# A decoder trunk in fp32: rotary angles and x*r on GpSimd and ScalarE, an earlier split of the first projections, and seam rows of 320 floats

## The chip, the core and the metric

The kernel runs on one core of a Trainium2 chip. What counts is the time of one execution on the device, in microseconds: the median of several runs. The engines are TensorE (PE; PEld is its weight load), VectorE (DVE), ScalarE (ACT), GpSimd (POOL) and SyncE (SP), which issues most DMAs.

## The reference

A trunk of two layers over 256 tokens of width 1024, batch 1, all in fp32. Each layer's shifts, scales and gates come from a conditioning vector c:

```python
for l in range(DEPTH):
    mod = c_act @ w_ada[l] + b_ada[l]
    shift1, scale1, gate1, shift2, scale2, gate2 = jnp.split(mod, 6, axis=-1)
    hdn = modulate(rmsnorm(x, norm1_g[l]), shift1, scale1)   # h * (1 + scale) + shift
    proj = hdn @ w_in[l]                                     # latents, q/k/v, gates
    ...                                                      # latent, stick-breaking, block attention
    x = x + gate1[:, None, :] * (merged @ w_out[l])
    hdn = modulate(rmsnorm(x, norm2_g[l]), shift2, scale2)
    ff = jnp.square(jax.nn.relu(hdn @ w_ff1[l])) @ w_ff2[l]
    x = x + gate2[:, None, :] * ff
return rmsnorm(x, final_norm_g)
```

Two of the three attentions turn part of q and k by rotary tables, cos and sin of position times frequency. The stick-breaking attention (sb) has none; its scores are z.

## The kernel before

x lies transposed in SBUF: eight slices (k = 0..7) of 128 features by 256 tokens. Weights come in blocks of 1 MB through three buffers `ws`, in a fixed order of jobs; `fetch` issues their DMAs on SyncE. Where a product must be as exact as fp32, each factor is split in a high half in fp32r and a low half that holds the rest, and three fp32r matmuls add up: high by high, high by low, low by high. `split_piece` splits a quarter of a block: ScalarE copies the high half `wh` (L184), VectorE subtracts to get `wl` (L185). Activations go the same way: `high` on ScalarE, `low` on VectorE, into `hh` and `hl` (in the trace both are parts of the tile act).

**The opening** (under `manual_schedule` in `trunk`, so every engine works in the order in which the code is written). VectorE computes the modulation by column: `ada_col` (L1097) multiplies a block of 128x1024 of w_ada by the conditioning row and sums it to one column; a pair of them gives scale (`gs`) and shift (`mod`) of one slice. `scaled(k)` makes x * gs * r on VectorE; for k from 4 on `gained(k)` does it on ScalarE from xr = x * r. The first eight jobs are the stick-breaking q, k and v projections. They run in four groups q of two slices each, as the columns become known: job 2q holds four blocks of the weights (1 MB), job 2q+1 two (0.5 MB). Groups below PLAIN_Q = 2 are plain: activations stay in fp32 (`hf`), weights are used unsplit, and TensorE does fp32 matmuls, each of two passes. Groups 2 and 3 are split. At the end of the opening the fp32 rows `hf` are split too, as later jobs need `hh` and `hl` for all slices.

Between the columns stands the rest: `table_angles`, a generator, which gives angle times frequency (L110), the count of turns (L111, L112), the reduction to one turn in three steps (L115) and a clamp (L116); `tables`, which on ScalarE takes absolute value and two sines and loads two function tables; and x * r for four slices (L1151).

**The seams** (`overlap`; one in the middle of each layer, one between the layers). The next projections start before the norm of x is known: `ahead` writes each new slice times its gain, split, into the tiles xh and xl, whose rows hold 256 tokens and two columns with the shift. `pre_mm` multiplies the weights by these rows of 258, and the norm factor is applied to the result. The sum of squares goes through TensorE: `Rms.sum` adds each term by an fp32 matmul with -1 (ssum), first `acc` with slices 0 to 5 and the late term of slice 6, later that of slice 7.

**The tail** (`tail`) does the last norm: squares of x by tiny matmuls (tsum), transposes of x * g (ft), then the scale. GpSimd multiplies x by the last gain g in the last seam (L813).

## Time and profile before

| what | us |
|---|---|
| median of 3 runs | 935.19 (934.09 to 935.22) |
| the profiled execution | 934.94 |
| its span in the trace | 933.2 |
| TensorE busy | 916.7 (98%) |
| VectorE busy | 731.0 (78%) |
| ScalarE busy | 600.5 (64%) |
| GpSimd busy | 8.7 (1%) |

The profiled execution's own time is 1.74 us above its span and 0.25 below the median of the runs. The busy shares are means over stages that differ: in the opening VectorE's share is higher than its mean, in the body TensorE's is.

### The profile page before, as it was taken

The numbers are of one execution on the slowest core, as the hardware profiler recorded it, in microseconds if no ns is written. First come the engines' busy times: TensorE is split into PE (matmuls) and PEld (weight loads), VectorE is DVE, ScalarE is ACT, GpSimd is POOL, SyncE is SP. The second block draws the span as 40 slices with busy tenths as digits, with TensorE's granted clock in tenths as the row PEclk, the third lists the DMA queues.
The fourth block names the chain that finished last, engine by engine and source line by source line (L and its number), as shares of the span: only waits on it lengthen the run. The fifth ranks groups of instructions, "written<-read, shape, count | busy, mean of one in ns | idle before, by whom it ended". The sixth has DMA issues, their size and how long they took to land.

```text
span 933.2 us, 19188 instructions
## 1 busy us (share of the span) xinstructions
PE 916.7 (98%) x7780; PEld 891.2 (96%) x7781; DVE 731.0 (78%) x1423; ACT 600.5 (64%) x1255; POOL 8.7 (1%) x14
## 2 busy tenths in 40 slices
PE   9999999999999999999999999999999999999997
PEld 6888999899999999999999999989999999999997
DVE  6979789887899986767888877889787989454553
ACT  3577678857676774645566667886667677564642
POOL 0000000000000000000000000000000000000002
PEclk9999999999999999999999999999999999999999
DMA  9956554664767488677947654655666637655531
GB/s 337 401 211 242 168 220 157 221 242 173 256 230 268 143 315 309 228 271 265 341 162 275 226 195 156 218 188 215 236 210 242 219 143 282 255 181 192 179 132 46
DMA packets 34074, 208.77 MB, mean 224 GB/s; under 512 B 3905, under 2 KB 4802, under 8 KB 11458
## 3 DMA queue, kind: packets, MB, share of 16 engines
q1 hardware_dynamic: 33696, 207.09, 62.0%
q8 instruction: 61, 1.00, 0.4%
q10 hardware_dynamic: 146, 0.26, 0.1%
q0 software_dynamic: 144, 0.20, 0.1%
q14 instruction: 27, 0.22, 0.1%
HBM read 206.49 MB, written 1.05 MB: 222 GB/s over the span
## 4 chain that ended last, share of the span: by engine, by line
PE 81%; DVE 9%; DMA 5%; ACT 4%; issue 1%; SPq 0%; DVEq 0%; ACTq 0%
PE ps L349 15%; PE ps L350 15%; PE ps L351 15%; PE ff L984 5%; PE ff L983 5%; PE ff L986 5%; PE pre L371 4%; DVE wl L185 3%; DMA ws<-win 3%; DMA adaw<-wada 2%; ACT wh L184 1%; PE po L476 1%; PE vps L349 1%; PE vps L350 1%; PE vps L351 1%; PE s L531 1%
## 5 line engine op out<-in xcount | busy, mean ns | idle before, releaser
L185 DVE TENSOR_TENSOR wl<-ws,wh 128x512 fp32r<-128x512 f32 (+1 forms) x592 | 378.8, 673 | 132.2 <-ACT wh L184 131.7
L184 ACT ACTIVATE wh<-ws 128x512 fp32r<-128x512 f32 (+1 forms) x592 | 337.3, 615 | 206.1 <-PE ps L350 108.3
L349 PE MATMUL ps<-act,wh 128*128 128x256 f32 x1120 | 312.4, 279 | 0.0
L351 PE MATMUL ps<-act,wl 128*128 128x256 f32 x1120 | 310.6, 277 | 0.0
L350 PE MATMUL ps<-act,wh 128*128 128x256 f32 x1120 | 310.5, 277 | 0.0
L350 PEld LDWEIGHTS ps<-act,wh 128*128 128x128 f32 x1120 | 211.0, 188 | 0.1
L349 PEld LDWEIGHTS ps<-act,wh 128*128 128x128 f32 x1120 | 210.5, 188 | 0.5 <-DVE wl L185 0.2
L351 PEld LDWEIGHTS ps<-act,wl 128*128 128x128 f32 x1120 | 210.4, 188 | 0.0
L983 PE MATMUL ff<-fh,wh 128*128 128x256 f32 x448 | 123.6, 276 | 0.0
L984 PE MATMUL ff<-fl,wh 128*128 128x256 f32 x448 | 123.6, 276 | 0.0
L986 PE MATMUL ff<-fh,wl 128*128 128x256 f32 x448 | 123.6, 276 | 0.0
L249 DVE SCALAR_TENSOR_TENSOR ws<-ws,cb 128x1024 f32<-128x1024 f32 x80 | 95.8, 1219 | 16.1 <-DMA ws<-wada 15.8
L986 PEld LDWEIGHTS ff<-fh,wl 128*128 128x128 f32 x448 | 84.1, 188 | 0.0
L983 PEld LDWEIGHTS ff<-fh,wh 128*128 128x128 f32 x448 | 84.1, 188 | 0.0
L984 PEld LDWEIGHTS ff<-fl,wh 128*128 128x128 f32 x448 | 84.1, 188 | 0.0
L551 ACT ACTIVATE e<-s,st 128x128 f32<-128x128 f32 (+1 forms) x64 | 25.9, 431 | 23.9 <-DVE st L546 18.7
L371 PE MATMUL pre<-xh,wh 128*128 128x258 f32 x96 | 28.3, 295 | 0.0
L350 PE MATMUL ps<-ml,wh 128*128 128x256 f32 x96 | 26.8, 281 | 0.5 <-DVE ml L242 0.5
L371 PE MATMUL pre<-xh,wl 128*128 128x258 f32 x96 | 27.1, 283 | 0.0
L371 PE MATMUL pre<-xl,wh 128*128 128x258 f32 x96 | 27.1, 282 | 0.0
L349 PE MATMUL vps<-wh,act 128*128 128x256 f32 x96 | 26.9, 280 | 0.0
L350 PE MATMUL vps<-wl,act 128*128 128x256 f32 x96 | 26.7, 278 | 0.0
(283 smaller groups left out, 1740.3 us busy)
## 6 DMA issues: line engine op xcount, KB each, us to landing
ws<-wff SPq DMA_DIRECT2D x64, 1024.0 KB, 4.9
ws<-win SPq DMA_DIRECT2D x50, 1024.0 KB, 4.9
ws<-wada SPq DMA_DIRECT2D x40, 1024.0 KB, 4.9
ws<-wo SPq DMA_DIRECT2D x12, 1024.0 KB, 4.9
adaw<-wada SPq DMA_DIRECT2D x16, 512.0 KB, 7.3
...
```

The source lines that it names most:

```text
L184: nc.scalar.activation(job.wh[:, a], job.ws[:, a], AF.Copy)
L185: nc.vector.tensor_sub(job.wl[:, a], job.ws[:, a], job.wh[:, a].bitcast(F32))
L249: nc.vector.scalar_tensor_tensor(w, w, 1.0, cb, op0=OP.mult, op1=OP.mult, accum_out=mods[l][:, 2 * b + i:2 * b + i + 1])
L349: nc.tensor.matmul(o, wh, ah, start=first, stop=False)
L350: nc.tensor.matmul(o, wh, al, start=False, stop=False)
L351: nc.tensor.matmul(o, wl, ah, start=False, stop=last)
L371: nc.tensor.matmul(ps[:, i, 0:258], w[:, c:c + 128], a[:, k, :], start=k == 0 and n == 0, stop=k == KT - 1 and n == 2, skip_group_check=True)
L476: nc.tensor.matmul(po[64 * h:64 * h + 64, u, o:256], v[:, k, vc:vc + 64], pT[:, h, c:c + n], start=k == 0, stop=k == 1, tile_position=(0, ...
L551: nc.scalar.activation(e[:, h, a:b], s[:, h, a:b], AF.Exp, scale=scale, bias=st[:, 4 + c:5 + c], accum_out=st[:, 8 + c:9 + c])
L983: nc.tensor.matmul(o, wh[:, c0:c0 + 128], fh[:, k, :], start=st, stop=False, skip_group_check=True)
L984: nc.tensor.matmul(o, wh[:, c0:c0 + 128], fl[:, k, :], start=False, stop=False, skip_group_check=True)
L986: nc.tensor.matmul(o, wl[:, c0:c0 + 128], fh[:, k, :], start=False, stop=en, skip_group_check=True)
```

## The change

The number of plain groups goes from two to one: group 1 is split, so it has `high` and `low` for slices 2 and 3, and its weights have high and low halves made by ScalarE and VectorE. hf has two rows instead of four, in a buffer of another pool, and the split at the end of the opening covers two slices.

The angles are made by ScalarE, the count of turns, the reduction (a multiplication and an addition in place of each combined instruction) and the clamp by GpSimd, and so is x * r. They are issued earlier. `low` for slices 4 and 6 stands directly behind `high`. Of job 6 two pieces are split ahead of the columns of slice 7; the single pieces that stood ahead of the second `low` of a group are dropped there. With group 1 split its two jobs come through the three buffers `ws` and not through the pools of the split weights, so the fetch of job 5 waits until job 2 has been split.

In the seams xh and xl become sixteen rows of 320 floats in three buffers (x0, x1, x2) and are read by their first 258. The late square of slice 6 is added to `acc` on VectorE, and one `sum` is left out. The tail has one term fewer in tsum and transposes two slices ahead where it was one.

```diff
--- before.py
+++ after.py
@@ -28,7 +28,7 @@
 MAGIC = 12582912.0
 
 WS, WB, AHEAD = 3, 3, 2
-PLAIN_Q = 2
+PLAIN_Q = 1
 EVERY = 3
 GAP_SB = 120, 72
 GAP_SM = 144, 72
@@ -97,7 +97,7 @@
 
     def table_angles():
         row = t256("row")
-        nc.vector.tensor_copy(row[0:1, :], posi)
+        nc.vector.tensor_scalar(row[0:1, :], posi, -1.0, None, op0=OP.mult)
         posf = mmps("posf")[:, 0, :]
         nc.tensor.matmul(posf, minus[0:1, :], row[0:1, :], start=True, stop=True)
         yield
@@ -107,13 +107,15 @@
         c3 = TWO_PI - c1 - c2
         ang, n = tab[:, 2:4, :], tab[:, 0:2, :]
         for i in range(2):
-            nc.vector.tensor_scalar(ang[:, i, :], posf, invs[:, i:i + 1], -1.0, op0=OP.mult, op1=OP.mult)
-        nc.vector.tensor_scalar(n, ang, 1.0 / TWO_PI, MAGIC, op0=OP.mult, op1=OP.add)
-        nc.vector.tensor_scalar(n, n, MAGIC, None, op0=OP.subtract)
+            nc.scalar.activation(ang[:, i, :], posf, AF.Copy, scale=invs[:, i:i + 1])
+        nc.gpsimd.tensor_scalar(n, ang, 1.0 / TWO_PI, MAGIC, op0=OP.mult, op1=OP.add)
+        nc.gpsimd.tensor_scalar(n, n, MAGIC, None, op0=OP.subtract)
         yield
+        t = t512("turns")
         for f in (c1, c2, c3):
-            nc.vector.scalar_tensor_tensor(ang, n, -f, ang, op0=OP.mult, op1=OP.add)
-        nc.vector.tensor_scalar(ang, ang, PI_SAFE, -PI_SAFE, op0=OP.min, op1=OP.max)
+            nc.gpsimd.tensor_scalar(t, n, -f, None, op0=OP.mult)
+            nc.gpsimd.tensor_add(ang, ang, t)
+        nc.gpsimd.tensor_scalar(ang, ang, PI_SAFE, -PI_SAFE, op0=OP.min, op1=OP.max)
         yield
 
     def tables():
@@ -293,10 +295,13 @@
                 nc.vector.tensor_add(self.acc, self.acc, sq[:, 0, :])
             self.i += 1
 
-        def square_late(self, a):
+        def square_late(self, a, add=False):
             sq = t256("sql")
             nc.scalar.activation(sq, a, AF.Square)
-            self.late.append(sq)
+            if add:
+                nc.vector.tensor_add(self.acc, self.acc, sq)
+            else:
+                self.late.append(sq)
 
         def sum(self, more=False):
             if self.ps is None:
@@ -368,7 +373,7 @@
             for i in range(2):
                 c = k * 256 + i * 128
                 for n, (w, a) in enumerate(((jb.wh, xg[0]), (jb.wh, xg[1]), (jb.wl, xg[0]))):
-                    nc.tensor.matmul(ps[:, i, 0:258], w[:, c:c + 128], a[:, k, :], start=k == 0 and n == 0,
+                    nc.tensor.matmul(ps[:, i, 0:258], w[:, c:c + 128], a[k][:, :S + 2], start=k == 0 and n == 0,
                                      stop=k == KT - 1 and n == 2, skip_group_check=True)
 
     def job(src, f, kts, act, done, ncol=256, before=None, pre=None):
@@ -818,13 +823,19 @@
             l2, gofs, sc, sh = (l, 56, 4, 3) if sec == 2 else (l + 1, 48, 1, 0)
             if k == 0:
                 rms["gs"] = gs = gain(l2, gofs, sc)
-                rms["xs"] = xh, xl = tuple(slot(n, F32R, (128, KT, S + 2)) for n in ("xh", "xl"))
-                m = mods[l2][:, sh * 8:sh * 8 + 8, None].to_broadcast([128, KT, 2])
-                split(xh[:, :, S:], xl[:, :, S:], m)
-            xh, xl = rms["xs"]
+                rows = [slot(n, F32R, (128, 6, 320)) for n in ("x0", "x1", "x2")]
+                rms["xs"] = [[rows[j // 6][:, j % 6, :] for j in range(i, i + KT)] for i in (0, KT)]
+                for t, p, k0, n in ((0, 0, 0, 6), (1, 0, 6, 2)):
+                    m = mods[l2][:, sh * 8 + k0:sh * 8 + k0 + n, None].to_broadcast([128, n, 2])
+                    nc.scalar.activation(rows[t][:, p:p + n, S:S + 2], m, AF.Copy)
+                for k0, n, t, p in ((0, 4, 1, 2), (4, 2, 2, 0), (6, 2, 2, 2)):
+                    m = mods[l2][:, sh * 8 + k0:sh * 8 + k0 + n, None].to_broadcast([128, n, 2])
+                    h = rows[0][:, k0:k0 + n, S:S + 2] if k0 < 6 else rows[1][:, 0:2, S:S + 2]
+                    nc.vector.tensor_sub(rows[t][:, p:p + n, S:S + 2], m, h.bitcast(F32))
+            xh, xl = (a[k] for a in rms["xs"])
             g = rms["gs"][:, k:k + 1]
-            nc.scalar.activation(xh[:, k, :S], x[:, k, :], AF.Copy, scale=g)
-            nc.vector.scalar_tensor_tensor(xl[:, k, :S], x[:, k, :], g, xh[:, k, :S].bitcast(F32),
+            nc.scalar.activation(xh[:, :S], x[:, k, :], AF.Copy, scale=g)
+            nc.vector.scalar_tensor_tensor(xl[:, :S], x[:, k, :], g, xh[:, :S].bitcast(F32),
                                            op0=OP.mult, op1=OP.subtract)
 
         def x_done(u, ps, sec):
@@ -841,7 +852,7 @@
             def go():
                 x_one(6 + i, ps, sec)
                 final(6 + i, sec)
-                rms["q"].square_late(x[:, 6 + i, :])
+                rms["q"].square_late(x[:, 6 + i, :], i == 0)
                 ahead(6 + i, sec)
             if i == 0:
                 go()
@@ -899,12 +910,12 @@
 
             total([q.acc] + q.late, True, False)
             q.late = []
-            turn(range(1))
+            turn(range(2))
             x_one(7, rms["end"], 5)
             q.square_late(x[:, 7, :])
             nc.vector.tensor_scalar(xg[:, 7, :], x[:, 7, :], gf[:, 7:8], None, op0=OP.mult)
             total(q.late, False, True)
-            turn(range(1, KT))
+            turn(range(2, KT))
             st = work.tile([128, 12], F32, name="st", tag="st", bufs=4)
             y, v, y2, z, r = (st[:, 2 * i:2 * i + 2] for i in range(5))
             sums = ts[:, :, 0]
@@ -928,7 +939,6 @@
             a, b = jobs[n:n + 2]
             split_to(n + 1, PIECES)
             pa, pb = atps("pre0"), atps("pre1")
-            rms["q"].sum(more=True)
             rms["last"]()
             pre_mm(a, pa, rms["xs"], range(3))
             rms["q"].sum()
@@ -1044,11 +1054,9 @@
                 for b in (4 + q, q):
                     nc.sync.dma_start(first_ada[b][:, i * D:i * D + D], wada[0, b][:, i * D:i * D + D])
 
-        for q in range(PLAIN_Q):
+        for q in range(3):
             ada_fetch(q)
             fetch_to(2 * q + 1)
-        ada_fetch(2)
-        fetch_to(5)
         ada_fetch(3)
         fetch_to(8)
         nc.sync.dma_start(msk, masks)
@@ -1086,6 +1094,7 @@
         for u in range(1, 4):
             rq.square(*x_pair(u), keep=True)
         rq.sum()
+        next(angles)
         warm(WARM[2])
         gs0 = cpool.tile([128, KT], F32, name="gs00")
         first_ht = {}
@@ -1131,12 +1140,15 @@
         ada_col(0, 0)
         r = rq.root(scalar=True)
         nc.gpsimd.dma_start(csr, signs)
-        hf.append(work.tile([128, 4, S], F32, name="hf", tag="v", bufs=2))
+        next(angles)
+        hf.append(work.tile([128, 2, S], F32, name="hf", tag="t512", bufs=4))
         plain_act(0, scaled(0))
         ada_col(4, 1)
         ada_col(0, 1)
         plain_act(1, scaled(1))
-        next(angles)
+        xr = work.tile([128, 4, S], F32, name="xr", tag="v", bufs=2)
+        for k in range(4, KT):
+            nc.gpsimd.tensor_mul(xr[:, k - 4, :], x[:, k, :], r)
         split_to(1, PIECES)
         for k in range(2):
             for i in range(2):
@@ -1144,26 +1156,26 @@
         for i in range(2):
             ada_col(5, i)
             ada_col(1, i)
-            plain_act(2 + i, scaled(2 + i))
-        next(angles)
-        xr = work.tile([128, 4, S], F32, name="xr", tag="v", bufs=2)
-        for k in range(4, KT):
-            nc.vector.tensor_mul(xr[:, k - 4, :], x[:, k, :], r)
+            t = scaled(2 + i)
+            high(2 + i, t)
+            low(2 + i, t)
+        for k in range(2, 4):
+            for i in (2, 3):
+                start_job(i, [k])
         tables()
-        start_job(2)
-        start_job(3)
         for q in (2, 3):
             k = 2 * q
             ada_col(4 + q, 0)
             ada_col(q, 0)
             ta = gained(k)
             high(k, ta)
+            low(k, ta)
+            if q == 3:
+                split_to(2 * q, 2)
             ada_col(4 + q, 1)
-            low(k, ta)
             ada_col(q, 1)
             tb = gained(k + 1)
             high(k + 1, tb)
-            split_to(2 * q, 1)
             low(k + 1, tb)
             if q == 2:
                 for i in (4, 5):
```

The order of VectorE around group 1, before: ht is a scaled slice, adaw a column reduction, gs and mod the columns, tab the angles, xr is x * r.

```order
L1107 SCALAR_TENSOR_TENSOR ht<-x,gs_226,rr 128x256
L1097 SCALAR_TENSOR_TENSOR adaw,mod_90<-adaw,cb 128x1024
L1102 SCALAR_TENSOR_TENSOR gs_226<-mod_90,onep,head 128x1
L1097 SCALAR_TENSOR_TENSOR adaw,mod_90<-adaw,cb 128x1024
L1099 TENSOR_TENSOR mod_90<-mod_90,head 128x1
L1107 SCALAR_TENSOR_TENSOR ht<-x,gs_226,rr 128x256
L115 SCALAR_TENSOR_TENSOR tab<-tab 128x512 x3
L116 TENSOR_SCALAR tab<-tab 128x512
L1151 TENSOR_TENSOR xr<-x,rr 128x256 x4
L1097 SCALAR_TENSOR_TENSOR adaw,mod_90<-adaw,cb 128x1024
```

And after, with the same two scaled slices, 2 and 3; act is the low half, wl the weights' low half.

```order
L1116 SCALAR_TENSOR_TENSOR ht<-x,gs_230,rr 128x256
L1131 SCALAR_TENSOR_TENSOR act<-ht,mod_90,act 128x256
L1106 SCALAR_TENSOR_TENSOR adaw,mod_90<-adaw,cb 128x1024
L1111 SCALAR_TENSOR_TENSOR gs_230<-mod_90,onep,head 128x1
L1106 SCALAR_TENSOR_TENSOR adaw,mod_90<-adaw,cb 128x1024
L1108 TENSOR_TENSOR mod_90<-mod_90,head 128x1
L1116 SCALAR_TENSOR_TENSOR ht<-x,gs_230,rr 128x256
L1131 SCALAR_TENSOR_TENSOR act<-ht,mod_90,act 128x256
L187 TENSOR_TENSOR wl<-ws,wh 128x512 x4
L187 TENSOR_TENSOR wl<-ws,wh 128x256 x4
L1106 SCALAR_TENSOR_TENSOR adaw,mod_90<-adaw,cb 128x1024
```

The table work and x * r are gone from VectorE, and two low halves and eight split pieces stand there.

VectorE in the fourth group before, from the first shift column of the group (slice 6) to the splits.

```order
L1099 TENSOR_TENSOR mod_90<-mod_90,head 128x1
L1097 SCALAR_TENSOR_TENSOR adaw,mod_90<-adaw,cb 128x1024
L1102 SCALAR_TENSOR_TENSOR gs_226<-mod_90,onep,head 128x1
L1122 SCALAR_TENSOR_TENSOR act<-ht,mod_90,act 128x256
L1097 SCALAR_TENSOR_TENSOR adaw,mod_90<-adaw,cb 128x1024
L1099 TENSOR_TENSOR mod_90<-mod_90,head 128x1
L185 TENSOR_TENSOR wl<-ws,wh 128x512
L1122 SCALAR_TENSOR_TENSOR act<-ht,mod_90,act 128x256
L185 TENSOR_TENSOR wl<-ws,wh 128x512 x3
L185 TENSOR_TENSOR wl<-ws,wh 128x256 x4
L242 TENSOR_TENSOR act<-hf,act 128x256 x4
```

And after.

```order
L1108 TENSOR_TENSOR mod_90<-mod_90,head 128x1
L1131 SCALAR_TENSOR_TENSOR act<-ht,mod_90,act 128x256
L187 TENSOR_TENSOR wl<-ws,wh 128x512 x2
L1106 SCALAR_TENSOR_TENSOR adaw,mod_90<-adaw,cb 128x1024
L1111 SCALAR_TENSOR_TENSOR gs_230<-mod_90,onep,head 128x1
L1106 SCALAR_TENSOR_TENSOR adaw,mod_90<-adaw,cb 128x1024
L1108 TENSOR_TENSOR mod_90<-mod_90,head 128x1
L1131 SCALAR_TENSOR_TENSOR act<-ht,mod_90,act 128x256
L187 TENSOR_TENSOR wl<-ws,wh 128x512 x2
L187 TENSOR_TENSOR wl<-ws,wh 128x256 x4
L244 TENSOR_TENSOR act<-hf,act 128x256 x2
```

Here the low half of slice 6 and two pieces of the split stand ahead of the last pair of columns; before, the low half stood between the two and no piece ahead of them.

GpSimd in the opening after; before it had there only the two first rows of the program and the DMA csr. turns is the product of a constant and the turn count.

```order
L111 TENSOR_SCALAR tab<-tab 128x512
L112 TENSOR_SCALAR tab<-tab 128x512
L1142 DMA csr<-signs 128x384
L116 TENSOR_SCALAR turns<-tab 128x512
L117 TENSOR_TENSOR tab<-tab,turns 128x512
L116 TENSOR_SCALAR turns<-tab 128x512
L117 TENSOR_TENSOR tab<-tab,turns 128x512
L116 TENSOR_SCALAR turns<-tab 128x512
L117 TENSOR_TENSOR tab<-tab,turns 128x512
L118 TENSOR_SCALAR tab<-tab 128x512
L1151 TENSOR_TENSOR xr<-x,rr 128x256 x4
```

Nine instructions over 512 elements and four over 256 have moved to GpSimd.

## Rows read from the trace of the kernel before

**Rows 1.** What TensorE waited for, 15 to 80 us: waiter <- awaited, us in total, times, longest

```profile
PE first L448 <- ACT wh L184: 2.5, 2, 2.2
...
PE z L517 <- DVE ll L242: 0.9, 1, 0.9
...
PE z L517 <- ACT lh L241: 0.4, 1, 0.4
```

**Rows 2.** Windows view, 16 to 47 us: span, busy (x count) of each engine, PEclk, DMA share, GB/s

```profile
core 0: us, PE busy (x) PEld busy (x) DVE busy (x) ACT busy (x) POOL busy (x), PEclk, DMA share, GB/s
16.00:47.00 31.00, 29.44 (x167) 25.81 (x165) 29.08 (x66) 12.76 (x23) 0.00 (x0) 1.00 1.04 400
```

**Rows 3.** Timeline of VectorE, 17 to 31 us: start, us, instruction, [idle before <- releaser]

```profile
17.77 0.86 DVE L110 TENSOR_SCALAR tab<-posf,head 128x256 f32<-128x256 f32 x2
...
19.47 1.22 DVE L1097 SCALAR_TENSOR_TENSOR adaw<-adaw,cb 128x1024 f32<-128x1024 f32 x1
...
25.73 2.14 DVE L115 SCALAR_TENSOR_TENSOR tab<-tab 128x512 f32<-128x512 f32 x3
...
29.59 1.22 DVE L1097 SCALAR_TENSOR_TENSOR adaw<-adaw,cb 128x1024 f32<-128x1024 f32 x1
```

**Rows 4.** Timeline of all engines, 46 to 54 us, the fourth group

```profile
46.88 0.16 DVE L1099 TENSOR_TENSOR mod<-mod,head 128x1 f32<-128x1 f32 x1
47.13 0.51 ACT L1119 ACTIVATE act<-ht,mod 128x256 fp32r<-128x256 f32 x1 [1.28 <-DVE mod L1099]
...
48.19 0.69 DVE L185 TENSOR_TENSOR wl<-ws,wh 128x512 fp32r<-128x512 f32 x1 [1.15 <-ACT wh L184]
...
48.21 0.51 PE L448 MATMUL first<-act,wh 128*128 128x256 f32 x2 [2.16 <-ACT wh L184]
48.80 0.48 DVE L1122 SCALAR_TENSOR_TENSOR act<-ht,mod,act 128x256 fp32r<-128x256 f32 x1
...
48.94 0.38 PE L448 MATMUL first<-act,wl 128*128 128x256 f32 x1 [0.22 <-DVE wl L185]
...
49.19 3.23 DVE L185 TENSOR_TENSOR wl<-ws,wh 128x512 fp32r<-128x512 f32 x7
...
52.34 1.42 DVE L242 TENSOR_TENSOR act<-hf,act 128x256 fp32r<-128x256 f32 x4
```

**Rows 5.** Timeline, 28 to 34.5 us: ScalarE's function tables, a high half, and a low half

```profile
28.37 0.63 ACT L121 ACTIVATE tab<-tab 128x512 f32<-128x512 f32 x1 [2.01 <-DVE tab L116]
...
32.87 0.51 ACT L1112 ACTIVATE ht<-xr,gs 128x256 f32<-128x256 f32 x1
33.41 0.51 ACT L1119 ACTIVATE act<-ht,mod 128x256 fp32r<-128x256 f32 x1
...
33.95 0.48 DVE L1122 SCALAR_TENSOR_TENSOR act<-ht,mod,act 128x256 fp32r<-128x256 f32 x1
```

**Rows 6.** Timeline of TensorE: plain products (32.99) and split passes (50 us)

```profile
32.99 3.62 PE L422 MATMUL first<-ws,hf 128*128 128x256 f32 x16
...
50.02 0.39 PE L448 MATMUL first<-act,wh 128*128 128x256 f32 x2
...
50.36 0.39 PE L448 MATMUL first<-act,wh 128*128 128x256 f32 x2
```

**Rows 7.** Timeline of SyncE's DMA issues, 27 to 37 us

```profile
27.30 3.56 SPq L161 DMA_DIRECT2D ws<-win  x4
```

**Rows 8.** Timeline at 908 us, and all eight instructions of line 290 (ns min/median/max)

```profile
908.25 2.35 POOL L813 TENSOR_SCALAR xg<-x,gf 128x256 f32<-128x256 f32 x2 [892.63 <-ACT wh L184]
...
909.81 0.61 DVE L290 TENSOR_TENSOR sacc<-sq 128x256 f32<-128x256 f32 x1
...
L290 DVE TENSOR_TENSOR sacc<-sq x8: 395/418/615, 112.8 to 909.8; 128x256 f32<-128x256 f32 x8
```

**Rows 9.** The chain that ended last, around the second seam: start, us, what

```profile
474.43 0.86 PE ssum L306 x4
...
477.92 9.35 PE pre L371 x78
```

**Rows 10.** Timeline of TensorE in the tail

```profile
924.08 0.59 PE L897 MATMUL tsum<-negs,sql 128*128 128x2 f32 x4
```

## The prediction

> **What bounds the kernel now.** I read the waits of TensorE first, then the windows view of the opening, then the timelines around the places that the change touches. TensorE is busy for 916.7 us of the 933.2 us span, so the time can change in only two ways: TensorE gets less to do, or its few waits grow or shrink. The waits between 15 and 80 us [rows 1] are the ones near the change: 2.2 us in the fourth group of projections, and 0.4 and 0.9 us later at the stick-breaking scores z. Behind these TensorE is what ends last nearly everywhere, so a shift that it carries out of 77 us reaches the end one for one.
>
> What TensorE waits for in the opening is VectorE. Between 16 and 47 us VectorE is busy for 29.08 of 31.00 us while the DMA engines show 1.04 [rows 2]; but the DMA data lies there before VectorE comes to it in this stretch, since no row in it names a DMA as what VectorE waited for. So I follow one chain: VectorE's work from the angles at 17.77 us [rows 3] to the eighth shift column at 46.88 us, the high half on ScalarE at 47.13, and TensorE at 48.21 [rows 4].
>
> **The change part by part: VectorE's work in the opening.** Out goes what stood between two column reductions: angles and turn counts, 17.77 to 19.47 = 1.70 us, and reduction, clamp and x*r, 25.73 to 29.59 = 3.86 us [rows 3]; together 5.56. In comes the split of group 1. The fourth group's split is the same eight pieces: 48.19 to 48.80 for the first and 49.19 to 52.34 for seven, 0.61 + 3.15 = 3.76 us; and two low halves at 0.39 (48.80 to 49.19) [rows 4], 0.78. Two pieces of job 6 now stand ahead of the eighth column, where none stood: 2 x 0.6 = 1.2. In all +5.74 - 5.56 = +0.2 us: the work removed from VectorE is given back whole.
>
> **Its waits.** A low half now stands straight behind its high half. The high half needs the shift column or the scaled row, takes 0.51 and the low starts 0.54 behind it (33.41 to 33.95) [rows 5]; a column or row is passed on in 0.25 (46.88 to 47.13) [rows 4]. For lows 2 and 3: 0.48 of the scaled row plus 0.54, less the 0.39 after which VectorE is free, about 0.65 each. For lows 5 and 6: 0.25 + 0.54 less 0.08 of the column's own issue, 0.71, and 0.13 more before the first split piece behind them. Low 4 waits for ScalarE's three table instructions and two loads of its function tables. They took 28.37 to 32.87 = 4.50 us [rows 5], and group 1's high splits now stand ahead of them, so I put them at 28.9 to 33.4; low 4 can start at 33.4 + 2 x 0.54 = 34.5, VectorE is there at 32.8: 1.7 us. With 0.13 in group 1 the new waits are 2 x 0.65 + 0.13 + 1.7 + 2 x 0.84 = 4.8 us. Queued behind each of them on VectorE are the next column reductions, for which the next group waits. Of VectorE's 1.92 us of idle time before [rows 2] I credit 1.5, which stood at the splits of the third group. So the eighth column comes at 46.88 + 0.2 + 4.8 - 1.5 = 50.4 us.
>
> **TensorE there.** The seventh high half is done at 50.4 + 0.25 + 0.51 = 51.2, the low at 51.75. Before, TensorE resumed at 48.94 behind its last small wait [rows 4]; now at 51.75 with 0.2 us of the sixth slice's products already behind it, so it leaves the group 2.6 us late. Group 1 saves it time: eight plain products took 3.62 us, 0.45 each, against 0.34 for three split passes (50.02 to 50.36) [rows 6], 24 x 0.11 = 2.7 us. I cost that gain at nothing, because TensorE then only waits longer for VectorE ahead of groups 2 and 3. VectorE's last splits end 1.25 us late, not 3.5: two pieces of job 6 are done ahead, and the final split of the fp32 rows has two instructions instead of four, 1.42 / 2 = 0.7 us less [rows 4]. So z's operands come 1.25 later and TensorE 2.6 later: the two waits there, 0.4 + 0.9 [rows 1], vanish. **Net +1.35 us.** If they stay instead, +2.6.
>
> **DMA.** Job 5's fetch has to wait for the last low split of job 2, which I put at 28.7 to 31 us. SyncE issued those fetches over 27.30 to 30.86 anyway [rows 7], and everything behind them on that queue (the last modulation blocks, jobs 6 to 8) moves by the same. Their data lies ready ahead of use, so: nothing, at worst 1 us if the fourth group's blocks come late.
>
> **GpSimd beside VectorE.** The trace has no such pair in the opening, only in the last seam: two GpSimd operations of 128x256 took 2.35 us, and a VectorE addition of two SBUF inputs beside them 0.61 us where the median of its eight is 0.418 [rows 8]. So one GpSimd operation of 256 elements costs such a VectorE instruction about 0.19 us. The change has nine operations of 512 elements and four of 256, 22 units. Four units fall before 15 us; at most 18 x 0.19 = 3.4 us hit VectorE. Some run while it waits anyway. I take ten, **+1.9 us**, range 0.3 (the one pair seen, and a little) to 3.4. The chain itself: 1.0 to 1.2 us for 256 elements, and I take 1.9 for 512, starting at about 11 us, when TensorE is through with the sum of squares: 11 + 9 x 1.9 = 28.1, about 29 us with the DMA that GpSimd issues between. ScalarE's tables wait for it, but would start at 28.9 + 1.9 = 30.8 in any case, so its length costs nothing up to there, and one for one beyond.
>
> The Trainium skill, "SBUF — State Buffer", section "Who interferes with whom", speaks against this part: a VectorE instruction with two SBUF inputs and a GpSimd instruction that reads SBUF shut each other out, the later one blocking fully. By that the addition above would have been held for the rest of a GpSimd operation, about 1 us; the row shows 0.2. It is rival B.
>
> **Seams and tail.** Three seams lose one fp32 pass over 128x256: two of them took 0.86 us [rows 9], so 3 x 0.43 = **-1.29 us**. The addition that replaces it (0.42 on VectorE) is covered, since both remaining passes now come behind 18 matmuls. The same matmuls read rows of 320 floats instead of 258. 78 of them took 9.35 us, 0.120 each [rows 9], against 0.113 for the split products of 256 columns in [rows 6]; their 258 columns explain 0.001. If the row length is the cause, 288 x 0.006 = -1.7 us. Among the single instructions slice 0, whose row stands where the 256-column rows do, is no faster than the others, so I take 0. The tail loses a group of four small matmuls, which took at most 0.59 us [rows 10], less the overlap of their modelled ends; the addition that replaces it may take some of it back: **-0.2** (0 to -0.59).
>
> **The sum.** 934.94 (the profiled execution) + 1.35 + 1.9 - 1.29 - 0.2 = 936.7. The median of the runs is 0.25 above the profiled one: 936.9 us, +0.19%. What a measurement can tell from no change is about 0.2%, 1.87 us: 933.3 to 937.1.
>
> **The rivals.**
> A, the forecast: 936.9, own range 935 to 938.5 (port cost 0.3 to 3.4). Chance 0.43, of which 0.25 within 0.2%, 0.17 slower, 0.01 faster.
> B, GpSimd blocks VectorE for whole operations. Seven operations of 512 elements, about 2 us each by [rows 8], would be added to a VectorE that has no slack [rows 2]; some 10 of the 14 us hit. It decides as soon as more than three operations block fully: 936.9 - 1.9 + 10 = 945. Against it stands the row of 0.61 us. Chance 0.1, slower.
> C, GpSimd's chain is slow. At 2.35 us for 512 elements, and VectorE holding it up, it ends at 35 instead of 29; the tables then start 4 us late and gained rows, highs and the third group follow: 941. Chance 0.14, slower.
> D, faster: GpSimd hardly disturbs (0.3), and the seam matmuls run at 0.113 with the longer rows: 936.9 - 1.6 - 1.7 = 933.6; with VectorE's waits of 0.7 partly covered, 932. Decides if rows of 258 cost what the longer pace suggests. Chance 0.21: 0.17 faster, 0.04 within.
> E, the two waits at z stay, or TensorE's longer waits bring its granted clock down from the 1.00 in [rows 2]: at half of it 1 us of products costs one more. 936.9 + 1.25 = 938.2. Chance 0.12: 0.1 slower, 0.02 within.
>
> **How the numbers follow.** Faster 0.17 + 0.01 = 0.18; within 0.25 + 0.04 + 0.02 = 0.31; slower 0.17 + 0.1 + 0.14 + 0.1 = 0.51. The range leaves out B and the slow end of C: 932 to 941.
>
> **What would show it.** The eighth shift column's row: near 52.3 (50.4 + 1.9) if the chain is right, 49 or earlier if the new waits are covered. VectorE's column reductions (1.22 us) between 15 and 30 us: 1.3 to 1.6 by A, 2 and more by B. The clamp's end on GpSimd: before 31 us by A, 35 by C. TensorE's wait in front of the fourth group: longer than 2.2 us, and none at z. Seam matmuls: 0.120 by A, 0.113 by D. Wrong would be above all the place of the waits behind the high halves: should ScalarE run ahead further than I think, the 4.8 us shrink and the forecast falls below the time before.

## The result: 0.73% slower

| | before | changed |
|---|---|---|
| median, six runs each | 935.21 us | 942.12 us |
| lowest to highest | 934.09 to 937.76 | 939.47 to 946.65 |
| profiled execution | 934.94 | 940.37 |
| its span | 933.2 | 938.6 |

The ratio is 1.0073, with an interval of 1.0050 to 1.0097: slower, clear of the 0.2% that can be told from no change. The direction and the part of the program were as forecast (936.9, slower more likely than not), but the median lies above the range (932 to 941); the profiled execution, which the traces below explain, lies inside it. The ratios leave out single runs more than 1.5% above the fastest of their kernel and are not ratios of the medians; medians and spreads are those of all runs. Medians of the kernel before lie between 934.7 and 936.3 from one comparison to the next, so each experiment is read against the runs of before beside it.

TensorE's waits between 15 and 80 us in the changed kernel (waiter, awaited, us in total, times, longest), against [rows 1]:

```profile
PE first L453 <- ACT wh L186: 7.2, 2, 5.9
PE first L453 <- ACT act L1128: 2.8, 1, 2.8
PE first L453 <- ACT hf L1125: 0.7, 1, 0.7
PE first L453 <- DVE wl L187: 0.2, 1, 0.2
```

Two waits at the weights' high halves, 5.9 and 1.3 us, and one of 2.8 us at the seventh high half; the two at z are gone, as forecast. The windows view of the same opening (columns as in [rows 2]):

```profile
15.00:47.00 32.00, 23.96 (x134) 21.75 (x135) 28.14 (x50) 14.51 (x28) 15.81 (x12) 0.89 0.93 334
47.00:62.00 15.00, 12.04 (x87) 11.64 (x86) 13.51 (x31) 8.46 (x21) 0.00 (x0) 0.89 0.69 273
```

VectorE is still busy for 28.14 of 32 us, though 5.56 us of its work went to GpSimd, which now shows 15.81. And the granted clock is 0.89 where it was 1.00.

What VectorE was busy with: its instructions between 16 and 32 us, by form (xcount, busy us, mean ns).

```profile
L1106 DVE SCALAR_TENSOR_TENSOR adaw<-adaw,cb 128x1024 f32<-128x1024 f32 x6 | 8.1, 1351 | 0.0
L1111 DVE SCALAR_TENSOR_TENSOR gs<-mod,onep,head 128x1 f32<-128x1 f32 x3 | 2.2, 721 | 0.1
L1108 DVE TENSOR_TENSOR mod<-mod,head 128x1 f32<-128x1 f32 x3 | 2.1, 698 | 0.1
L1131 DVE SCALAR_TENSOR_TENSOR act<-ht,mod,act 128x256 fp32r<-128x256 f32 x2 | 2.0, 1008 | 1.2 <-ACT act L1128 1.2
L1116 DVE SCALAR_TENSOR_TENSOR ht<-x,gs,rr 128x256 f32<-128x256 f32 x3 | 2.0, 657 | 0.0
```

An addition of one column (mod) takes 698 ns on average; in [rows 4] it took 0.16 us. Its timeline beside GpSimd's shows why:

```profile
16.22 0.48 DVE L1111 SCALAR_TENSOR_TENSOR gs<-mod,onep,head 128x1 f32<-128x1 f32 x1
16.63 1.21 DVE L1106 SCALAR_TENSOR_TENSOR adaw<-adaw,cb 128x1024 f32<-128x1024 f32 x1
...
17.89 1.10 DVE L1108 TENSOR_TENSOR mod<-mod,head 128x1 f32<-128x1 f32 x1
...
20.97 1.13 DVE L1111 SCALAR_TENSOR_TENSOR gs<-mod,onep,head 128x1 f32<-128x1 f32 x1
...
24.69 1.53 DVE L1131 SCALAR_TENSOR_TENSOR act<-ht,mod,act 128x256 fp32r<-128x256 f32 x1 [0.58 <-ACT act L1128]
...
16.09 1.49 POOL L116 TENSOR_SCALAR turns<-tab 128x512 f32<-128x512 f32 x1
17.67 1.30 POOL L117 TENSOR_TENSOR tab<-tab,turns 128x512 f32<-128x512 f32 x1
...
20.81 1.27 POOL L117 TENSOR_TENSOR tab<-tab,turns 128x512 f32<-128x512 f32 x1
...
24.67 1.27 POOL L117 TENSOR_TENSOR tab<-tab,turns 128x512 f32<-128x512 f32 x1
26.02 0.67 POOL L118 TENSOR_SCALAR tab<-tab 128x512 f32<-128x512 f32 x1
```

17.67 + 1.30 = 18.97 and 17.89 + 1.10 = 18.99: the column addition ends where GpSimd's addition ends. So does the second pair (22.08 and 22.10); the low half ends 0.28 us behind GpSimd's addition (25.94, 26.22), with the rest of its own work. Beside an addition, which reads two tensors, VectorE does not run at a lower speed; it stands still until GpSimd's instruction is over. Beside a GpSimd instruction with one input it is held for less. The multiplication recorded from 16.09 to 17.58 lengthened a column of scale from 0.22 to 0.48 us, and then VectorE's column reduction at 16.63 ran at its usual 1.21 us inside the same record. Such an instruction takes 0.67 us where VectorE does not stand in its way (26.02), so here it did some of the waiting itself. How the two take turns inside it was not tried.

GpSimd's chain itself was not late: the clamp was through at 26.69, and ScalarE came to the tables at 34.80, behind its splits of group 1. VectorE's column reductions took 1.35 us on average, which is the sign that the prediction gave for its own price; the stops sat in the short instructions.

The fourth group in the changed kernel, against [rows 4]:

```profile
56.36 0.16 DVE L1108 TENSOR_TENSOR mod<-mod,head 128x1 f32<-128x1 f32 x1
56.62 0.51 ACT L1128 ACTIVATE act<-ht,mod 128x256 fp32r<-128x256 f32 x1 [0.83 <-DVE mod L1108]
...
57.18 0.91 PE L453 MATMUL first<-act,wh 128*128 128x256 f32 x2 [2.82 <-ACT act L1128]
...
59.05 0.63 PE L453 MATMUL first<-act,wh 128*128 128x256 f32 x2
...
59.69 0.63 PE L453 MATMUL first<-act,wh 128*128 128x256 f32 x2
...
62.40 0.39 PE L453 MATMUL first<-act,wh 128*128 128x256 f32 x2
...
67.25 0.70 PE L490 MATMUL z<-sbqk 64*128 64x256 f32 x4
```

The eighth column comes at 56.36 instead of 46.88, 9.5 us later. Behind the wait a product of three passes takes 0.64 us (59.05 to 59.69), 0.21 us for 256 columns: the 1.2 GHz level, after 2.8 us in which TensorE had done nothing; by 62.4 it is back. TensorE comes to z at 67.25, where the kernel before was there at 57.25:

```profile
57.25 0.70 PE L485 MATMUL z<-sbqk 64*128 64x256 f32 x4
```

The chain at the first seam, changed kernel, then before:

```profile
306.15 2.17 PE pre L376 x18
308.31 0.86 PE ssum L311 x4
309.18 9.44 PE pre L376 x78
```

```profile
298.37 0.86 PE ssum L306 x4
299.23 2.19 PE pre L371 x18
301.42 0.43 PE ssum L306 x2
301.86 9.35 PE pre L371 x78
```

TensorE enters it 7.8 us late, and the seam takes 2.17 + 0.86 + 9.44 = 12.47 instead of 12.84 us (298.37 to 311.21): 0.37 gained. The other two seams gain the same, together 1.1 us.

### The profile page after: what moved, and what is told of

The parts are those of the page before. It is cut to its first block, busy times and chain, and to the rows that moved or that the text cites. A ratio compares the mean times of both kernels' runs of the same rounds, so it can differ in the third digit from the quotient of the medians.

```text
span 938.6 us, 19258 instructions
## 1 busy us (share of the span) xinstructions
PE 915.6 (98%) x7794; PEld 892.1 (95%) x7795; DVE 737.8 (79%) x1429; ACT 604.7 (64%) x1266; POOL 26.1 (3%) x27
## 3 DMA queue, kind: packets, MB, share of 16 engines
q1 hardware_dynamic: 33696, 207.09, 61.6%
HBM read 206.49 MB, written 1.05 MB: 221 GB/s over the span
## 4 chain that ended last, share of the span: by engine, by line
PE 83%; DVE 10%; ACT 3%; DMA 2%; issue 1%; SPq 0%; DVEq 0%; ACTq 0%
PE ps L354 15%; PE ps L355 15%; PE ps L356 15%; PE ff L993 5%; PE ff L994 5%; PE ff L996 5%; PE pre L376 4%; DVE wl L187 3%; PE po L481 1%; PE vps L354 1%; PE vps L355 1%; PE vps L356 1%; DVE adaw L1106 1%; DMA ws<-win 1%; PE z L522 1%; PE s L536 1%
## 5 line engine op out<-in xcount | busy, mean ns | idle before, releaser
L187 DVE TENSOR_TENSOR wl<-ws,wh 128x512 fp32r<-128x512 f32 (+2 forms) x600 | 383.0, 673 | 131.1 <-ACT wh L186 130.3
L186 ACT ACTIVATE wh<-ws 128x512 fp32r<-128x512 f32 (+2 forms) x600 | 340.6, 613 | 207.6 <-PE ps L355 108.5
L376 PE MATMUL pre<-x,wh 128*128 128x258 f32 x192 | 35.6, 287 | 0.0
L818 POOL TENSOR_SCALAR xg<-x,gf 128x256 f32<-128x256 f32 x7 | 7.3, 1051 | 889.5 <-ACT wh L186 882.3
L453 PE MATMUL first<-act,wh 128*128 128x256 f32 x96 | 21.3, 322 | 10.1 <-ACT wh L186 7.2
L376 PEld LDWEIGHTS pre<-x,wh 128*128 128x128 f32 x192 | 30.1, 191 | 0.2
L453 PEld LDWEIGHTS first<-act,wh 128*128 128x128 f32 x96 | 17.8, 227 | 11.1 <-ACT wh L186 7.8
```

Source lines behind the costliest of these rows:

```text
L186: nc.scalar.activation(job.wh[:, a], job.ws[:, a], AF.Copy)
L187: nc.vector.tensor_sub(job.wl[:, a], job.ws[:, a], job.wh[:, a].bitcast(F32))
L376: nc.tensor.matmul(ps[:, i, 0:258], w[:, c:c + 128], a[k][:, :S + 2], start=k == 0 and n == 0, stop=k == KT - 1 and n == 2, skip_group_che ...
L453: nc.tensor.matmul(ps[:, i, :], w[:, c:c + 128], a[:, k, :], start=i == 0 and k == 0 and n == 0, stop=k == KT - 1 and n == 2, skip_group_c ...
```

## The experiments

Theory after the result: (1) VectorE stands still for GpSimd's instructions, 5.5 us in all instead of 1.9; (2) the waits behind the high halves, as forecast; (3) TensorE's clock falls in the longer waits; (4) the seams bring their 1.1 us. The rival was that the waits alone carry the loss and GpSimd does little.

**GpSimd's part alone, and the changed kernel without it.** gps is the kernel before with

```diff
-            nc.vector.tensor_scalar(ang[:, i, :], posf, invs[:, i:i + 1], -1.0, op0=OP.mult, op1=OP.mult)
+            nc.scalar.activation(ang[:, i, :], posf, AF.Copy, scale=invs[:, i:i + 1])
...
-            nc.vector.scalar_tensor_tensor(ang, n, -f, ang, op0=OP.mult, op1=OP.add)
+            nc.gpsimd.tensor_scalar(t, n, -f, None, op0=OP.mult)
+            nc.gpsimd.tensor_add(ang, ang, t)
...
-            nc.vector.tensor_mul(xr[:, k - 4, :], x[:, k, :], r)
+            nc.gpsimd.tensor_mul(xr[:, k - 4, :], x[:, k, :], r)
```

> The kernel before with only the rotary angles and x*r moved to ScalarE and GpSimd; groups, splits and seams as before. Theory (VectorE stands still for whole GpSimd operations, 5.5 us in the changed kernel, about as much as the 5.56 us of work taken off it): eighth shift column at 46.5 to 47.5 us, time within 1 us of before. Rival (VectorE loses 1.9 us, as the prediction took it): eighth column at about 43.5, TensorE's wait of 2.2 us at the fourth group gone, time about 932.5.

936.63 against 935.41, ratio 1.0010 (0.9994 to 1.0026). The eighth column:

```profile
46.82 0.16 DVE L1102 TENSOR_TENSOR mod<-mod,head 128x1 f32<-128x1 f32 x1
```

5.56 us of work left VectorE and its chain ends where it did (46.88), though its first scaled row came 0.9 us earlier. 1.7 us went into waits for modulation blocks, the rest, about 4.7 us, into longer instructions, above all shift and scale columns of 0.66 and 0.90 us on average. The prediction's price of 1.9 us is refuted.

nogps is the changed kernel with those instructions taken out:

```diff
-        nc.gpsimd.tensor_scalar(n, ang, 1.0 / TWO_PI, MAGIC, op0=OP.mult, op1=OP.add)
-        nc.gpsimd.tensor_scalar(n, n, MAGIC, None, op0=OP.subtract)
...
-            nc.gpsimd.tensor_mul(xr[:, k - 4, :], x[:, k, :], r)
```

> The changed kernel without GpSimd's work in the opening: the count of turns, the reduction, the clamp and x*r are left out (the sines take the scaled angles, the gained rows take x), all else as changed. Theory (GpSimd's hold on VectorE is the missing term): eighth shift column at about 50.6 us instead of 56.4, VectorE's small instructions back at 0.16 and 0.22 us, time 935 to 936.5. Rival (the waits behind the high halves are the loss): eighth column at 54 or later, time above 939.

The eighth column came at 51.48, 0.9 us later than expected but far from 54, while the time was 945.79 against 935.41 (1.0105, 1.0084 to 1.0126): the column goes with the theory, the time does not. The trace put the surplus far from the opening. In the second layer's feed-forward stage TensorE, never idle and at a granted clock of 1.00, did 256 columns in 117.8 ns where the changed kernel's profile has 113.3. That pace became a question of its own (below), and the pair was repeated with the seams of before.

> The changed kernel with rows of 258 in the seams. Theory (about 5 us of the loss are the opening, the rest is the pace behind the seams): median 939 to 940, lowest run as that of the changed kernel, none above 943. Rival (all of the loss comes from the opening): median within 1 us of the changed kernel's 942.1 and the same spread.

after258 (rows of 258 in the changed kernel): 943.23 against 935.66, 1.0075 (1.0059 to 1.0091), six runs between 941.5 and 944.4. sum258 (below), run beside it, differs from it by the opening alone and gave 934.14: the opening costs 9.1 us. So the expectation of 939 to 940 was wrong, and so was the bound of 943 for single runs; the rival, that all of the loss comes from the opening, is the nearer one.

> The changed kernel with rows of 258 in the seams and without GpSimd's work in the opening (turn count, reduction, clamp and x*r left out, as in the run nogps). Theory (GpSimd's hold on VectorE costs 5 us of the opening, and the longer wait at the seventh slice lets the granted clock fall): eighth column at 51 to 51.5 us, no half-clock stretch behind it, 936 to 938, against 943.2 with that work. Rival (the waits behind the high halves carry most of the loss): 940 or more.

nogps258: 939.76 against 935.37, 1.0036 (1.0019 to 1.0053). Its instructions between 16 and 32 us:

```profile
L1093 DVE SCALAR_TENSOR_TENSOR adaw<-adaw,cb 128x1024 f32<-128x1024 f32 x8 | 9.8, 1219 | 0.2 <-DMA adaw<-wada 0.2
...
L1103 DVE SCALAR_TENSOR_TENSOR ht<-x,gs,rr 128x256 f32<-128x256 f32 x3 | 1.4, 479 | 0.0
...
L1118 DVE SCALAR_TENSOR_TENSOR act<-ht,mod,act 128x256 fp32r<-128x256 f32 x2 | 1.0, 485 | 1.2 <-ACT act L1115 1.2
L1098 DVE SCALAR_TENSOR_TENSOR gs<-mod,onep,head 128x1 f32<-128x1 f32 x4 | 0.9, 220 | 0.1
...
L1095 DVE TENSOR_TENSOR mod<-mod,head 128x1 f32<-128x1 f32 x3 | 0.5, 160 | 0.1
```

The differences to the changed kernel, times the counts there, are 6 x 0.13 + 3 x 0.50 + 3 x 0.54 + 2 x 0.52 + 3 x 0.18 = 5.5 us, and the eighth column stands at 50.94 instead of 56.35. VectorE's waits for the high halves are the same in both (4.7 us in six waits), so it is the hold that went. In time that is worth 0.0075 - 0.0036, about 3.6 us, less than the column, and above my 936 to 938: its runs lie in two heaps, 935.5 to 937.6 and 939.6 to 941.3. In the profile it had a wait of 3.1 us at the values of the latent attention (mvps, from 168 us) where after258 has 2.2 and the kernel before 1.5, and a granted clock of 0.66 in the 5 us around its end. Why that wait grows here was not tried.

**What of GpSimd's work shuts VectorE out.** fills258 is nogps258 with

```diff
+        for i in range(13):
+            nc.gpsimd.memset(t, float(i))
```

on a tile of 128x1024.

> As nogps258, with 13 GpSimd fills of 128x1024 (writes only, no SBUF operand read) from about 15 us on in place of its work. Theory (what shuts VectorE out is GpSimd reading SBUF): VectorE's column instructions stay at 0.16 and 0.22 us beside the fills, eighth column and time as in nogps258. Rival (any GpSimd access to SBUF holds VectorE): small instructions of 0.4 us and more, eighth column 2 us or more later than in nogps258.

```profile
15.36 13.09 POOL L115 MEMSET turns<- 128x1024 f32 x13
```

```profile
22.73 0.16 DVE L1099 TENSOR_TENSOR mod<-mod,head 128x1 f32<-128x1 f32 x1
22.81 0.48 DVE L1107 SCALAR_TENSOR_TENSOR ht<-x,gs,rr 128x256 f32<-128x256 f32 x1
```

GpSimd writes without a pause from 15.4 to 28.4 us, and VectorE's instructions have their own lengths. 937.72 against 935.37 (1.0022, 1.0006 to 1.0038). The eighth column was 1.9 us later than in nogps258, against the expectation, with 2.1 us of waits for modulation blocks in that stretch; no instruction was longer. Whether the fills delayed those blocks was not tried. So it is GpSimd's reading, and not its writing, that shuts VectorE out. The Trainium skill, "SBUF — State Buffer", section "Who interferes with whom", states just this (a VectorE instruction with two SBUF inputs and a GpSimd instruction that reads SBUF exclude each other, one that only writes does not): the traces agree, 1.10 us for a 0.16 us addition beside a reading instruction, 0.16 beside a fill. The prediction gave the rule with the later one blocking fully. GpSimd's additions do that here, but a VectorE reduction of 1.21 us ran inside the 1.49 us record of a one-input instruction (16.09), and there the measurement decides.

**The waits behind the high halves.** lows258 puts the low halves back behind the next work, in group 1 too (left out here), and with them the places of the split pieces:

```diff
             high(k, ta)
-            low(k, ta)
-            if q == 3:
-                split_to(2 * q, 2)
             ada_col(4 + q, 1)
+            low(k, ta)
             ada_col(q, 1)
             tb = gained(k + 1)
             high(k + 1, tb)
+            split_to(2 * q, 1)
             low(k + 1, tb)
```

> The changed kernel with rows of 258 and the low halves back behind the next column reduction (or the first split piece), one piece of each group's split ahead of the second low as before; GpSimd's work as changed. Theory (the low halves' waits are real but smaller than GpSimd's share): VectorE's waits for the high halves fall from 4.7 to under 1.5 us, eighth column at 52 to 54 us, 940 to 941.5. Rival (the waits only move): eighth column within 1 us of 56.4, 943.

940.07 against 935.37, 1.0050 (1.0031 to 1.0069): 2.3 us better than after258 by the ratios. VectorE's waits in the opening, lows258 and then after258:

```profile
DVE wl L187 <- ACT wh L186: 3.4, 3, 1.2
DVE adaw L1100 <- DMA adaw<-wada: 0.4, 1, 0.4
```

```profile
DVE act L1125 <- ACT act L1122: 4.7, 6, 1.6
```

In after258 the 4.7 us are six waits, 4.1 of them ahead of the eighth column. Counted as the forecast did, from the time when VectorE is free to the low half or the piece behind it, those five are 0.66 and 0.67 for lows 2 and 3 (forecast 0.65), 1.73 for low 4 (1.7), 0.84 and 0.86 for lows 5 and 6 (0.84), with 0.13 in group 1: 4.9 for 4.8.

In lows258 they are gone, and 2.3 us of waits at split pieces and 0.4 for a modulation block stand ahead of the column instead; the third of the 3.4 us comes behind it. So the waits shrank by 1.4 us only, while the column came at 51.23, 5.1 us earlier. Most of the rest has other reasons: the first scaled row came 1.0 us earlier (13.53 for 14.55), two split pieces, 1.2 us, no longer stand ahead of the column, and the stops beside GpSimd add up to 4.6 us where after258 has 5.5. So this run moves more than the low halves. That the waits lie in VectorE's chain is shown; what they alone cost in time is not.

**The clock.** warm and warm258 put idle matmuls into TensorE's two long waits:

```diff
+        for _ in range(24):
+            nc.tensor.matmul(wfill, wsrc[:, :128], wsrc, start=True, stop=True)
```

(12 of them at the second place.)

> The changed kernel with 24 idle matmuls of 512 columns in TensorE's wait ahead of group 1 and 12 in its wait ahead of the seventh slice. Theory (TensorE's granted clock falls in the long waits and costs 1.5 us after the second): products at 0.34 us from 57 to 62 us instead of 0.64, about 940.5, and runs that lie closer together than the 7 us of the changed kernel. Rival (VectorE sets the end of the opening in any case): 941.5 to 942.5.

> The changed kernel with rows of 258 in the seams and idle matmuls in TensorE's two long waits (24 and 12 of 512 columns). Theory (the granted clock's fall behind the second wait costs about 1.3 us): 941.5 to 942.3 against 943.2 without them, products behind the second wait at 0.34 to 0.36 us instead of 0.64. Rival (VectorE's chain sets the end there): 943 to 943.5.

```profile
55.38 2.76 PE L1188 MATMUL wfill<-csr 128*128 128x512 bf16 x12
...
56.15 0.51 ACT L1128 ACTIVATE act<-ht,mod 128x256 fp32r<-128x256 f32 x1 [0.83 <-DVE mod L1108]
...
57.79 0.59 PE L453 MATMUL first<-act,wh 128*128 128x256 f32 x2
...
59.03 0.40 PE L453 MATMUL first<-act,wh 128*128 128x256 f32 x2
...
59.39 0.40 PE L453 MATMUL first<-act,wh 128*128 128x256 f32 x2
```

In warm the products behind the second wait take 0.36 us instead of 0.64, and from the first of them to z TensorE needs 66.55 - 57.79 = 8.8 us instead of 10.1: 1.3 us, as reckoned. The times do not show it: warm gave 946.98 against 935.41 (1.0110, 1.0077 to 1.0144; six runs, 940.2 to 950.5), warm258 942.74 against 936.29 (1.0078, 1.0056 to 1.0100), no better than after258's 1.0075. The profile says why these runs could not show it: in the changed kernel TensorE starts 0.56 us behind the start of the high half (56.62, 57.18), in warm 1.64 us behind it (56.15, 57.79), because the idle matmuls still run. They ate 1.1 of the 1.3 us (0.6 in warm258); from the eighth column to z TensorE's way is 10.65 us in warm and 10.89 in the changed kernel. Fewer idle matmuls were not tried. So the clock's 1.3 us are seen in the opening of a profile; that they reach the end is not shown.

**The seams, and two paces of TensorE.** seams is the kernel before with the change's seam and tail part; sum258 has all of that but the rows; rows320 has the rows in their three buffers alone; rows322 and rows288 are seams with one number changed:

```diff
-                rows = [slot(n, F32R, (128, 6, 320)) for n in ("x0", "x1", "x2")]
+                rows = [slot(n, F32R, (128, 6, 322)) for n in ("x0", "x1", "x2")]
```

> The kernel before with the seam and tail part of the change alone (rows of 320, one pass of the sum of squares fewer, the tail's order); the opening as before. Theory (the opening carries the whole loss, the seams bring what three passes cost): 1.1 to 1.3 us faster than before, about 934.0, with the seam matmuls at 0.120 us as before. Rival (the longer rows cost or save something of their own): more than 2 us away from before, and a pace of the seam matmuls that differs from 0.120.

> The kernel before with the rest of the seam and tail change, one pass of the sum of squares fewer at each seam, and rows of 258 as before. Theory (rows of 258 bring the quick pace back): about 934.0, 1.1 to 1.3 us under before, runs as close together as those of before, 113 ns behind both seams. Rival (the order of the sums sets the pace): single runs in steps of 6.7 us as with the whole seam change, median 937 to 941.

> The kernel before with only the seam rows changed to 320 floats in three buffers; the sums of squares as before. Theory (TensorE has two paces, 113 and 118 ns for 256 columns; rows of 258 bring it back to the quick one at each seam, rows of 320 leave it in the one it came in): single runs in steps of about 6.7 us, some at 934 and some at 941 and 948, median 937 to 941; in the trace the feed-forward stage behind a seam has the pace of the stretch ahead of it. Rival (the lost break by a pass of the sum of squares between the seam matmuls is what matters): like before, 934 to 936, and 113 ns behind both seams of the profile.

> The run seams with one number changed: rows of 322 floats instead of 320, so that each row starts 8 bytes further against a 64-byte grid, as rows of 258 do. Theory (what brings TensorE back to the quick pace is that the rows' starts move against the grid): about 934, runs as close as those with rows of 258, 113 ns behind both seams. Rival (the three buffers, or the missing early pass of the sum, let the slow pace through): steps of 6.7 us, median 937 to 941 as in the run seams.

> The run seams with rows of 288 floats: again a multiple of 64 bytes (18 x 64), but another length than 320. Theory (the rows' starts against a 64-byte grid decide): spread in steps of about 6.7 us as in the run seams, median 937 to 941. Rival (320 itself, or the span of memory that the rows cover, decides): close runs at 934 to 935 as with 322.

> The run seams once more (rows of 320, one pass of the sum fewer), now on the same chip as the two runs beside it; rows of 288, also a multiple of 64 bytes, ran close together on another chip, so the 64-byte grid is not it. Theory (320 floats, 5 x 256 bytes, keep every row at the same place of a 256-byte grid, and that lets the slow pace through, on any chip): steps of about 6.7 us, median 937 to 941. Rival (the chip of that run decided): close runs at 933 to 936.

> The run rows322 once more, on the same chip as seams_again. Theory (row starts that move on a 256-byte grid bring the quick pace back): 933 to 935, at most one run in ten above 939. Rival (the chip decides): the same spread as seams_again.

> The run rows320 once more (rows of 320, the sums of squares as before, so an fp32 pass stands directly ahead of the seam matmuls), on the same chip as the other two. Theory (the pass ahead of the seam matmuls brings the quick pace back, as it seemed in 11 of 12 runs): close runs at 934 to 937. Rival (rows of 320 let the slow pace through whatever the sums): steps of 6.7 us as in seams_again.

| run | this / before, us | ratio (interval) | lowest to highest; runs above 939 |
|---|---|---|---|
| seams | 939.71 / 935.41 | 1.0022 (0.9997 to 1.0048) | 932.4 to 948.0; 8 of 12 |
| seams_again | 933.67 / 934.72 | 0.9995 (0.9979 to 1.0011) | 932.4 to 940.3; 2 of 12 |
| sum258 | 934.14 / 935.66 | 0.9984 (0.9969 to 1.0000) | 932.4 to 938.1; 0 of 12 |
| rows320 | 935.93 / 935.66 | 1.0008 (0.9987 to 1.0029) | 933.8 to 946.5; 1 of 12 |
| rows320_again | 934.95 / 934.72 | 1.0008 (0.9995 to 1.0020) | 934.0 to 940.0; 1 of 12 |
| rows322 | 934.51 / 935.37 | 0.9991 (0.9978 to 1.0005) | 932.0 to 939.4; 1 of 12 |
| rows322_again | 933.65 / 934.72 | 0.9990 (0.9978 to 1.0002) | 932.0 to 937.7; 0 of 12 |
| rows288 | 933.83 / 936.29 | 0.9977 (0.9962 to 0.9993) | 931.4 to 939.6; 1 of 12 |

The seam and tail part without the rows is worth what was forecast: sum258 is 1.5 us under before, for 1.29 + 0.2, with an interval that just reaches no change. What goes with the high median of seams is the pace. The windows view counts matmuls: ahead of the first seam (287 to 297) and in the first layer's feed-forward stage (325 to 450), in seams_again, then in rows322_again. rows320_again has 87 and 1105.

```profile
287.00:297.00 10.00, 10.00 (x87) 10.00 (x86) 9.89 (x22) 7.57 (x17) 0.00 (x0) 1.00 0.74 257
325.00:450.00 125.00, 125.00 (x1064) 125.00 (x1062) 88.53 (x155) 67.16 (x127) 0.00 (x0) 1.00 0.74 270
```

```profile
287.00:297.00 10.00, 10.00 (x87) 10.00 (x86) 9.94 (x23) 7.58 (x18) 0.00 (x0) 1.00 0.77 279
325.00:450.00 125.00, 125.00 (x1106) 125.00 (x1105) 92.99 (x164) 69.16 (x131) 0.00 (x0) 1.00 0.78 282
```

All three come to the seam at the slow pace (87 matmuls in 10 us). Two leave it at the quick one, 1106 and 1105 in 125 us, 0.113 each; seams_again goes on at 1064, 0.1175 each. Over a feed-forward stage of 170 us that is 170 x 42 / 1106 = 6.5 us: the step between the heaps of single runs. The clock is 1.00 and TensorE never idle in both, so neither view names a cause.

By the spacing of single matmuls in all profiles but that of seams, where a stretch ahead of the first or third seam is slow, rows of 258 and 322, and rows of 320 with the early pass of the sum, let the quick pace follow in eleven of eleven; rows of 320 without that pass (seams_again, nogps, warm) in two of four. That is few cases, and the spreads beside it do not settle it. On the chip of seams, 8 of its 12 runs lay above 939 us, but only 1 of 23 of before and 1 of 10 of gps, so the seam part matters there; on another chip the same kernel had 2 of 12, against none of 12 for rows of 322 and none of 28 for before. Rows of 288 (18 x 64 bytes) had 1 of 12 above 939, on a chip where rows of 320 had 2, and their profile comes to no seam at the slow pace, so the theory of a grid of 64 bytes is neither shown nor refuted. That 320 floats are five times 256 bytes and the other rows are not multiples of that would fit too, but no second multiple was run. What sets the pace stays open.

**A version that beats both.** The kernel before with the seam and tail part and 2.4 us of the rotary work in VectorE's waits for its first modulation blocks, its functions in the same order on VectorE itself (the generator stops at two more places for it, left out here):

```diff
+        next(angles)
         ada_col(4, 0)
+        next(angles)
         ada_col(0, 0)
+        next(angles)
         r = rq.root(scalar=True)
```

> The kernel before with rows of 258, one pass of the sum of squares fewer at the seams, and about 2.4 us of the rotary work on VectorE put into its waits for the first modulation blocks (before 14 us). Theory (the chain of VectorE's work sets the opening one for one until TensorE's waits are used up): eighth column 1.5 to 2.4 us earlier than 46.9, TensorE's wait at the fourth group under 1 us, about 932 to 932.5. Rival (the DMAs of the modulation blocks take over as the limit): eighth column unchanged, 934.

> The kernel before with the seam and tail change, rows of 322 floats, and about 2.4 us of the rotary work in VectorE's early waits. Theory (the terms add: seams 1.2, rows harmless, VectorE's chain 1.2 us shorter): 932.5 to 934, runs close together. Rival (the quick pace is lost in some runs all the same): a spread above 6 us.

early258: 933.90 against 935.66, 0.9979 (0.9967 to 0.9992). early322: 933.22 against 936.29, 0.9966 (0.9954 to 0.9978), six runs within 1.8 us. The eighth column in early258 came 1.2 us earlier, not 1.5 or more, and TensorE's wait at the fourth group stayed:

```profile
45.70 0.16 DVE L1104 TENSOR_TENSOR mod<-mod,head 128x1 f32<-128x1 f32 x1
```

```profile
47.03 0.64 PE L454 MATMUL first<-act,wh 128*128 128x256 f32 x2 [1.86 <-ACT wh L187]
```

An earlier column lets the group before it end earlier as well, so the wait moves with it instead of shrinking: the expectation that it falls under 1 us was wrong. And the product in that row takes 0.64 us: TensorE ran at the 1.2 GHz level until 50.6, with a granted clock of 0.77 from 44 to 50 us where the kernel before has 1.00. Behind that it came to z at 57.24, where before it was there at 57.25; in early322's profile it came at 58.79. The times are lower, but the seam and tail part alone gives most of that: 0.9984 in sum258 beside early258's 0.9979, 0.9977 in rows288 (rows of 288) beside early322's 0.9966. What is left for the moved work, 0.5 and 1.0 us, lies inside the intervals.

## Why the prediction failed

**Right.** VectorE's chain is what sets the opening, and the work balance of +0.2 us holds: nogps258, without GpSimd, has its eighth column at 50.94 where the chain without port cost gave 50.4. The waits behind the high halves came to 4.9 us for 4.8, each near its own price. VectorE's last splits end 7.2 us late for a column 9.5 us late, 2.3 us made up, as forecast (1.25 for 3.5; the terms shown there give only 1.9, the rest is a shorter wait for the first piece). The two waits at z vanished. The gain of the split products of group 1 was rightly put at nothing, as TensorE waited 5.9 us ahead of them. Seams: 1.1 us by the trace for 1.29, and the seam matmuls kept 0.12 us.

**Wrong: the price of GpSimd beside VectorE.** The step "one GpSimd operation of 256 elements costs such a VectorE instruction about 0.19 us" misread [rows 8]. The 2.35 us of two operations there were taken as their length; at least 1 us of it must be GpSimd waiting for VectorE, as an instruction of twice the size takes 0.67 us with one input and 1.28 with two where VectorE does not stand in its way (timeline above). And the 0.2 us of the 0.61 us addition were taken as what any GpSimd operation costs. They came from a one-input instruction that was already running, and such instructions cost 0.3 to 0.4 us in the opening; an addition of 512 elements holds VectorE to its end, 0.9 to 1.05 us more for one instruction. One row of a rare pair gave the price of all. 1.9 us were put in, 3.4 as the upper bound, and 5.5 came. Rival B had the mechanism nearer and the price wrong the other way (10 us): it counted 2 us for each operation, the same misreading.

**Wrong: the clock and the start.** TensorE's longer waits were seen, but the half-clock stretch behind them stood only in rival E; 1.3 us at z by the traces. The length of the wait does not decide it alone: behind 2.16 us the kernel before kept its clock [rows 4], behind 1.86 early258 lost it. And the first scaled row came at 14.56 us instead of 14.23, 0.3 us. The angles, now on ScalarE ahead of the norm factor, may be the cause, but with the opening of before that row lies between 13.97 (seams) and 14.63 (sum258), so it is not shown.

Together: 1.35 + 1.9 were put in up to the first seam, and 7.8 us came. 3.6 of the 4.5 us between them are GpSimd, 1.3 the clock, 0.3 the start; that is 0.7 too much. Of this I can place about 0.5: between z and the seam the changed kernel's profile happens to have fewer matmuls at the slow pace. What stands behind the seam differs little in the two profiles, 7.8 - 3 x 0.37 = 6.7 to 5.4 at the end of the span; of the 1.3 us between, 1.0 lie in the second layer's attention stage, where the changed profile again has fewer slow matmuls, and 0.3 in the tail. This explains the profiled executions, 5.4 us apart; the medians are 6.9 apart, and no slower execution of the changed kernel was profiled. That the spread rose from 3.7 to 7.2 us fits the slow pace that rows of 320 can let through (after258 had 2.9), but six runs each do not show it.

**The range** ended at 941 because the bounds of the port's price came from the same misread row. A bound must come from another mechanism, not from twice the same reading: VectorE held for all of GpSimd's chain, which I put at 17 us, would have been one.
